# Second attention: the window branch transposed on TensorE a block later, queries asked for one head ahead

## The chip, the cores and the metric

The kernel runs on one core of a Trainium2 chip. The metric is the device time of one execution in microseconds (us). Runs of one kernel agree within some tenths of a per cent.

## The reference

One transformer layer on 1024 tokens of width 1024: a feed-forward half-step, a token mixer, a second feed-forward half-step, and a final norm. The mixer adds a differential attention (8 heads) and a sparse attention (16 heads of width 64 in 2 groups). The sparse attention is the one touched here; it is the second that the kernel computes. Cut to what matters:

```python
def nsa(q, k_cmp, v_cmp, k_slc, v_slc, k_win, v_win, gate_logits, ...):
    ...                                   # o_cmp: attention to compressed keys
    s = jnp.where(mask, q @ ks * scale, NEG_INF)       # selected blocks; 16 of 16 are selected
    o_slc = softmax(s) @ v_slc                         # so: causal attention to all tokens
    s = jnp.where(window mask, q @ kw * scale, NEG_INF) # the last WIN = 512 tokens
    o_win = softmax(s) @ v_win
    g = jax.nn.sigmoid(gate_logits)
    return g[..., 0:1] * o_cmp + g[..., 1:2] * o_slc + g[..., 2:3] * o_win
```

So each query block of 128 tokens meets two key ranges: block i has i+1 key tiles of 128 in the selected branch, and min(i+1, 5) in the window branch.

## The kernel before

The program is one stream of tile operations on one core; a scheduler places them on the engines' queues when the program is built, by its own estimate of times, and each engine then works through its queue in that order. SP issues all DMAs. The stages are: first feed-forward; preliminary projections; `da_phase`, the first (differential) attention; `ns_phase`, the second attention; projections; second feed-forward.

`ns_phase` loops over 2 groups, 4 pairs of heads each, the two halves H of the sequence, the two heads of the pair (`par`), and 4 query blocks i of the half: 128 blocks in all. For each block `ns_scores` makes, for the selected branch and then for the window branch:

- `scores` (L822 to L831): two matmuls for each piece into a PSUM tile `S` (three buffers), mask and row maximum on DVE (L829), exponential with row sums on ACT into `Ps` (selected) or `Pw` (window), two buffers each.
- the reciprocal of both row sums and the gate, in `l` (L983, L984).
- the scaled probabilities as two f16 halves, high and low, in a tile `ph` (two buffers for each branch): the high half on POOL for the selected branch (L993) and on ACT for the window branch (L991), the low half on DVE (L994).
- a DMA transpose of that tile from SBUF to SBUF (L996) into `pT` (four buffers), issued by SP.

`ns_pv` multiplies the transposed tiles with the values (`vt`, f16 with both halves side by side, L1011) into a PSUM tile `o`, three blocks later (`NS_LAG = 3`). The first product of four blocks takes the compressed branch `pc` (L1005). After four blocks `ns_fold` (L1019 on ACT, L1020 on DVE) folds `o` into `y`, and after both heads of a pair `ns_out` splits `y` and stores it (L1028). At the top of each head the queries `qt` are loaded (L1342, two tiles, two buffers each), at the top of each pair and half `pc` (L1335).

Between the blocks `fill.step()` puts pieces of independent matrix products (L51 to L53, "the filler", into `gm`) into the program: the gate projections and the first attention's output projection.

`da_phase` computes a similar attention without DMA transposes: there the probabilities are scaled on POOL (L863) and DVE (L865), transposed on PE (L877) and split from PSUM on ACT (L88) and DVE (L84).

Of the kernel before, what the change touches and what calls it, by code (L numbers as in the profile page):

```python
# [7 lines left out]
F32 = mybir.dt.float32  # L8
F32R = mybir.dt.float32r
F16 = mybir.dt.float16  # L10
AF = mybir.ActivationFunctionType
ALU = mybir.AluOpType
# [4 lines left out]
P = 128  # L17
T = 1024
TB = 512
# [3 lines left out]
KD = 8  # L23
# [63 lines left out]
def split(nc, hi, lo, src):  # L87
    nc.scalar.activation(out=hi, in_=src, func=AF.Copy)  # L88
    return lo_of(nc, lo, src, hi)


def load_w(K, src):
    if K.fill is not None:
        return K.fill.take()
    return load_w_parts(K, src, 1)()
# [171 lines left out]
def ffn_up(K, w13, w2, ctxt, ctx0, gi, first):  # L267
# [45 lines left out]
    with ctx:  # L313
# [33 lines left out]

        n0, n1 = NPLAIN, NF // 2
        r = load(n0)
        X, sv = first_product(r)  # L350
        for fp in range(n0, n1):
# [314 lines left out]
def gate_unit(K, c):  # L666
    nc = K.nc
    w = load_w(K, K.A["win"][C_GATE + c])
    for tb in range(NTB):
        ps = K.gm.tile([P, TB], F32, tag="gm", name="gm")  # L670
        yield from fill_gemm(K, ps, w, K.h[tb])
        vt = K.vtp.tile([P, TB], F32, tag="vt", name="vt")
        nc.vector.tensor_tensor(out=vt, in0=ps, in1=K.R[tb], op=ALU.mult)
        nc.sync.dma_start(out=K.s_mix[tb][c % KD][:, c // KD], in_=vt)


def pda_load(K):
    nc = K.nc
    K.y = []
    for tb in range(NTB):  # L680
        K.y.append([])
        for k in range(KD):
            t = [K.hp.tile([P, TB], F32R, tag=f"{n}{tb}_{k}", name="yl") for n in ("hi", "lo")]
            for i in range(2):
                nc.sync.dma_start(out=t[i].bitcast(F32), in_=K.s_yda[tb][k][:, i])
            K.y[tb].append(t)


def pda_unit(K, d):
    nc = K.nc  # L690
    if d == 0:
        pda_load(K)
    w = load_w(K, K.A["wda"][d])
    for tb in range(NTB):
        ps = K.gm.tile([P, TB], F32, tag="gm", name="gm")
        yield from fill_gemm(K, ps, w, K.y[tb])
        vt = K.vtp.tile([P, TB], F32, tag="vt", name="vt")
        nc.scalar.activation(out=vt, in_=ps, func=AF.Copy)
        nc.sync.dma_start(out=K.s_mix[tb][d][:, 2], in_=vt)


def compress_load(K, kv):
# [257 lines left out]
def ns_load_values(K):  # L960
    K.nv = {}
    vt = [pool.tile([P, 2, 8, P], F16, tag=tag, name="vt") for pool, tag in ((K.kp, "v0"), (K.mp, "m42"))]
    for g in range(2):
        for br in range(2):
            t = vt[g][:, br]
            K.nc.sync.dma_start(out=t, in_=K.s_v2[br][g])
            K.nv[g, br] = t


def ns_scores(K, hd, i, qt, g):  # L970
    nc = K.nc
    w = P * (i + 1)
    b0 = max(0, i - 4)
    ww = P * (i + 1 - b0)
    l = K.sm.tile([P, 2], F32, tag="l", name="l")
    nm = K.sm.tile([P, 2], F32, tag="nm", name="nm")
    qs = [t[:, (i % 4) * P:(i % 4 + 1) * P] for t in qt]
    p0 = K.pp.tile([P, T], F32, tag="P0", name="Ps")
    p1 = K.pp.tile([P, 5 * P], F32, tag="P1", name="Pw")
    scores(K, [(q, K.nk[g, 0], 0) for q in qs], w, K.slab[:, T - w:T], nm[:, 0:1], p0, l[:, 0:1])  # L980
    mk = K.slab[:, T - ww:T] if i < 4 else K.wslab
    scores(K, [(q, K.nk[g, 1], b0 * P) for q in qs], ww, mk, nm[:, 1:2], p1, l[:, 1:2])
    nc.vector.reciprocal(out=l, in_=l)  # L983
    nc.vector.tensor_tensor(out=l, in0=l, in1=K.G[:, i, hd * 3 + 1:hd * 3 + 3], op=ALU.mult)  # L984
    ts = []
    for c, (p, n) in enumerate(((p0, w), (p1, ww))):
        half = K.hp16.tile([P, n // P, 2, P], F16, tag=f"H{c}", name="ph")
        hi, lo = half[:, :, 0], half[:, :, 1]
        pv, lc = p[:, 0:n].rearrange("p (j k) -> p j k", k=P), l[:, c:c + 1]
        if c:  # L990
            nc.scalar.activation(out=hi, in_=pv, func=AF.Copy, scale=lc)  # L991
        else:
            nc.gpsimd.tensor_scalar(out=hi, in0=pv, scalar1=lc, scalar2=1.0, op0=ALU.mult, op1=ALU.mult)  # L993
        nc.vector.scalar_tensor_tensor(out=lo, in0=pv, scalar=lc, in1=hi, op0=ALU.mult, op1=ALU.subtract)  # L994
        t = K.tp.tile([P, n // P, 2, P], F16, tag=f"T{c}", name="pT")
        nc.sync.dma_start_transpose(out=t.rearrange("p j a q -> p (j a) q"), in_=half.rearrange("p j a q -> p (j a q)"))  # L996
        ts.append(t)
    return ts


def ns_pv(K, i, ts, o, pc, g, par):
# [22 lines left out]
def ns_out(K, pr, H, y):  # L1024
    nc = K.nc
    yo = K.mp.tile([P, 2, TB], F32R, tag="rl", name="yo")
    split(nc, yo[:, 0], yo[:, 1], y)
    nc.sync.dma_start(out=K.s_yns[H][pr], in_=yo.bitcast(F32))  # L1028


def order_after(K, inst, first):
    if first is not None:
        K.tc.add_manual_dep(inst.ins, first.ins.name,
                            mybir.DependencyInfo(mybir.DependencyClass.NoSync, mybir.DependencyReason.DATA),
                            reason="order the filler's weights")


class Filler:
# [22 lines left out]
    def load(self):  # L1061
        n = len(self.loaded)
        if n < len(self.srcs):
            st = self.K.wst.tile([P, KD, P], F32, tag="wst", name="wst")
            order_after(self.K, self.K.nc.sync.dma_start(out=st, in_=self.srcs[n]), self.last)
            self.loaded.append(st)

    def split(self):
# [147 lines left out]
def gate_units(K, cs):  # L1216
    return [lambda c=c: gate_unit(K, c) for c in cs]
# [22 lines left out]
NS_LAG = 3  # L1240
# [63 lines left out]
def ns_phase(K):  # L1304
    nc = K.nc
    K.low = LOW_NS
    with ExitStack() as ctx:
        K.wslab = open_pool(K, ctx, "wsl", 1).tile([P, 5 * P], F32, name="wslab")
        nc.sync.dma_start(out=K.wslab, in_=K.A["wslab"])
        K.qp, K.kp, K.pcp = open_pool(K, ctx, "nq", 2), open_pool(K, ctx, "nk", 1), open_pool(K, ctx, "npc", B_NPC)  # L1310
        K.pp, K.sm, K.tp, K.op = (open_pool(K, ctx, "np", B_NP), open_pool(K, ctx, "nsm", 6), open_pool(K, ctx, "nt", B_NT),
                                  open_pool(K, ctx, "no", B_NO))
        K.hp16 = open_pool(K, ctx, "nh", B_NH)
        K.sp = open_pool(K, ctx, "sp2", 3, True)
        K.ops = open_pool(K, ctx, "o2", 1, True)
        K.gm = open_pool(K, ctx, "gm2", 1, True)
        fill = K.filler
        fill.pace(8 + 16 + KD, PACE_NS)
        ns_load_values(K)
        pend = []  # L1320

        def finish(hd, i, res, st, g, par):
            if i % 4 == 0:
                K.o = K.ops.tile([P, TB], F32, tag="o", name="o")
            ns_pv(K, i, res, K.o, st[0], g, par)
            if i % 4 == 3:
                ns_fold(K, g, par, K.o, st[1])
                if par:
                    ns_out(K, hd // 2, i // 4, st[1])

        for g in range(2):
            for pr in range(4 * g, 4 * g + 4):
                for H in range(2):
                    pc = K.pcp.tile([P, 2, TB], F32R, tag="pc", name="pc")
                    nc.sync.dma_start(out=pc.bitcast(F32), in_=K.s_pc[pr][H])  # L1335
                    y = K.op.tile([P, TB], F32, tag="y", name="y")
                    for par in range(2):
                        hd = pr * 2 + par
                        qt = []
                        for z in range(2):  # L1340
                            t = K.qp.tile([P, TB], F32R, tag=f"q{z}", name="qt")
                            nc.sync.dma_start(out=t.bitcast(F32), in_=K.s_qns[hd // 4][z:z + 2, :, hd % 4, :, H * TB:(H + 1) * TB]  # L1342
                                              .rearrange("h a d t -> (h a) d t"))
                            qt.append(t)
                        for i in range(4 * H, 4 * H + 4):
                            res = ns_scores(K, hd, i, qt, g)
                            fill.step()
                            pend.append((hd, i, res, (pc, y), g, par))
                            if len(pend) > NS_LAG:
                                finish(*pend.pop(0))  # L1350
        fill.end()
        for p in pend:
            finish(*p)


def proj(K, open_x, after):
# [54 lines left out]
def body(tc, A, out):  # L1411
    nc = tc.nc
    K = Ctx()
    K.tc, K.nc, K.A = tc, nc, A
    K.low, K.vv, K.gate, K.fill, K.seen = 0, {}, None, None, {}
    K.h, K.acc, K.R = [None] * 2, [None] * 2, [None] * 2
    with ExitStack() as ctx:
# [172 lines left out]
```

## Time and profile before

| | |
|---|---|
| time, median of 3 runs | 3113.57 us (3110.08 to 3121.97) |
| the profiled execution's own time | 3118.4 us |
| its span in the profile | 3116.6 us |
| granted TensorE clock, mean over the span | 0.944 |
| PE busy (share of the span) | 2811.5 us (90%) |
| DVE busy | 1982.2 us (64%) |
| ACT busy | 1213.8 us (39%) |
| POOL busy | 902.3 us (29%) |
| second attention | about 1490 to 2250 us |

How to read it: PE is TensorE's matmuls, PEld its weight loads, DVE VectorE, ACT ScalarE, POOL GpSimd, SP the engine that issues the DMAs. A busy share is an average over stages with different limits; a change in one stage is read from that stage. A line such as `PE o L1011 <- DMA pT<-ph: 118.1, 66, 12.3` says that PE, before the instruction that writes `o` at line 1011, idled 118.1 us in total, 66 times, at most 12.3 us, until the DMA that fills `pT` from `ph` had landed. The granted clock is the share of full speed that TensorE got. Across the whole page PE is busy in nine tenths or more of most slices, and in five to eight tenths in the slices of the second attention.

### The profile page before, as it was taken

What the parts mean: (1) busy time and instruction counts of PE and PEld (TensorE: products, weight loads), DVE (VectorE), ACT (ScalarE), POOL (GpSimd) and SP (SyncE); (2) the same over time, 40 slices, a digit from 0 to 9 for tenths busy, and PEclk for the clock granted to TensorE, in tenths of its full rate; (3) what the DMA queues carried; (4) which work ended last, traced back from release to release, by engine and by line L of the source; (5) the groups of instructions that cost most, each with busy time, mean ns of one, the idle gap of its engine ahead of it and who ended that gap; (6) DMA issues with size and microseconds to landing.
All of it is one profiled execution on the core that took longest, in us unless ns stands there. A gap on an engine that the chain in (4) does not pass through costs nothing. (4 is left out here: it accounts for less than half of the span.)

```text
span 3116.6 us, 39466 instructions
## 1 busy us (share of the span) xinstructions
PE 2811.5 (90%) x14080; PEld 2309.3 (74%) x14080; DVE 1982.2 (64%) x3108; ACT 1213.8 (39%) x2024; POOL 902.3 (29%) x637
## 2 busy tenths in 40 slices
PE   9999999999999999898677765777899999999998
PEld 7887788887887778787566654566678788777886
DVE  8765675666784677677566664566533676576656
ACT  6322233533332454455444442445432532222443
POOL 4366550000242223222111110111152326655101
PEclk9999999999999999999778876788899999999999
DMA  3354467654456454444689888889972225545854
GB/s 135 122 202 173 176 206 266 221 160 138 150 218 211 156 181 171 171 152 149 125 169 165 166 163 214 165 159 176 215 292 106 88 102 188 174 172 187 276 199 142
DMA packets 491238, 545.32 MB, mean 175 GB/s; under 512 B 299424, under 2 KB 319136, under 8 KB 491040
## 3 DMA queue, kind: packets, MB, share of 16 engines
q1 hardware_dynamic: 491040, 542.79, 59.5%
q8 instruction: 111, 1.82, 0.2%
q14 instruction: 87, 0.71, 0.1%
HBM read 312.52 MB, written 160.96 MB: 152 GB/s over the span
## 5 line engine op out<-in xcount | busy, mean ns | idle before, releaser
L822 PE MATMUL S<-kt,qt 128*128 128x320 f32 (+5 forms) x1152 | 288.6, 374 | 85.7 <-DMA qt<-sqn 46.0
L51 PE MATMUL gm<-hi,whi 128*128 128x512 f32 x880 | 357.7, 407 | 6.6 <-ACT whi L88 3.9
L52 PE MATMUL gm<-lo,whi 128*128 128x512 f32 x880 | 353.2, 401 | 0.0
L53 PE MATMUL gm<-hi,wlo 128*128 128x512 f32 x880 | 353.0, 402 | 0.1
L822 PEld LDWEIGHTS S<-kt,qt 128*128 128x128 f32 x1152 | 210.9, 211 | 119.9 <-DMA qt<-sqn 53.9
L829 DVE CUSTOM_DVE_ANT_0 S<-S,slab 128x896 f32<-128x896 f32 (+7 forms) x320 | 224.3, 710 | 116.7 <-PE S L822 114.6
L993 POOL TENSOR_SCALAR ph<-Ps,l 128x384 f16<-128x384 f32 (+7 forms) x128 | 113.2, 885 | 623.6 <-DVE l L984 292.8
L326 PE MATMUL Y<-tf,whi 128*128 128x512 f32 x864 | 271.3, 396 | 12.7 <-DVE u L369 9.5
L1011 PE MATMUL o<-pT,vt 128*128 128x128 f16 x2112 | 170.8, 240 | 118.6 <-DMA pT<-ph 118.1
L84 DVE TENSOR_TENSOR wlo<-st,whi 128x1024 fp32r<-128x1024 f32 x154 | 197.6, 1303 | 117.5 <-ACT whi L88 117.2
L1011 PEld LDWEIGHTS <-vt 128*128 128x128 f16 x2112 | 145.1, 109 | 154.6 <-issue 153.0
L52 PE MATMUL acc<-wlo,whi 128*128 128x512 f32 (+1 forms) x628 | 242.8, 387 | 0.0
L51 PE MATMUL acc<-whi 128*128 128x512 f32 (+1 forms) x628 | 242.6, 386 | 0.0
L53 PE MATMUL acc<-whi,wlo 128*128 128x512 f32 (+1 forms) x628 | 242.3, 388 | 0.0
L88 ACT ACTIVATE whi<-st 128x1024 fp32r<-128x1024 f32 x154 | 159.9, 1056 | 187.3 <-PE acc L53 117.3
L326 PEld LDWEIGHTS Y<-tf,whi 128*128 128x128 f32 x864 | 161.8, 189 | 55.0 <-issue 10.9
L51 PEld LDWEIGHTS gm<-hi,whi 128*128 128x128 f32 x880 | 171.7, 195 | 41.3 <-ACT whi L88 4.5
L53 PEld LDWEIGHTS gm<-hi,wlo 128*128 128x128 f32 x880 | 171.0, 194 | 37.1 <-DVE wlo L84 0.6
L52 PEld LDWEIGHTS gm<-lo,whi 128*128 128x128 f32 x880 | 171.7, 195 | 32.0
L84 DVE TENSOR_TENSOR wlo<-a,whi 128x1024 fp32r<-128x1024 f32 x90 | 135.6, 1509 | 73.8 <-ACT whi L88 73.0
L84 DVE TENSOR_TENSOR wlo<-wst,whi 128x1024 fp32r<-128x1024 f32 x103 | 134.5, 1309 | 75.3 <-ACT whi L88 65.3
L326 PE MATMUL Y<-tf,wlo 128*128 128x512 f32 x432 | 170.1, 395 | 0.0
(321 smaller groups left out, 6533.5 us busy)
## 6 DMA issues: line engine op xcount, KB each, us to landing
wst<-in_win_dram SPq DMA_DIRECT2D x55, 512.0 KB
sw<-w2s SPq DMA_DIRECT2D x44, 512.0 KB
st<-sw SPq DMA_DIRECT2D x88, 256.0 KB
st<-saT SPq DMA_DIRECT2D x88, 256.0 KB
a<-in_f1w_dram SPq DMA_DIRECT2D x36, 512.0 KB
a<-in_f2w_dram SPq DMA_DIRECT2D x36, 512.0 KB
st<-saB SPq DMA_DIRECT2D x66, 256.0 KB
qt<-sq SPq DMA_DIRECT2D x128, 128.0 KB
```

The source lines that it names most:

```text
L51: first = nc.tensor.matmul(out, lhsT=w[0][:, wk], rhs=x[0], start=start, stop=False, skip_group_check=skip)
L52: nc.tensor.matmul(out, lhsT=w[0][:, wk], rhs=x[1], start=False, stop=False, skip_group_check=skip)
L53: nc.tensor.matmul(out, lhsT=w[1][:, wk], rhs=x[0], start=False, stop=stop, skip_group_check=skip)
L84: return nc.vector.tensor_tensor(out=lo, in0=src, in1=hi.bitcast(F32), op=ALU.subtract)
L88: nc.scalar.activation(out=hi, in_=src, func=AF.Copy)
L326: K.mark = nc.tensor.matmul(o, lhsT=w[a][:, m * h + k], rhs=x[k][b], start=start and k == 0 and i == 0, stop=k == h - 1 and i == 2, skip_g ...
L822: K.last = nc.tensor.matmul(S[:, o:o + n], lhsT=q, rhs=k[:, k0 + c:k0 + c + n], start=i == 0, stop=i == 1)
L829: nc.vector.tensor_tensor_reduce(out=sv, in0=sv, in1=mv, scale=-0.125, scalar=BIG, op0=ALU.add, op1=ALU.min, accum_out=nm)
L993: nc.gpsimd.tensor_scalar(out=hi, in0=pv, scalar1=lc, scalar2=1.0, op0=ALU.mult, op1=ALU.mult)
L1011: nc.tensor.matmul(dst, lhsT=K.nv[g, br][:, j], rhs=ts[br][:, j - b0, hl], start=False, stop=i % 4 == 3 and (br, j, hl) == (1, i, 1), skip ...
```

## The change

In the second attention only the selected branch is still transposed by DMA. For the window branch POOL scales the probabilities in place (f32), and a new function `ns_window` transposes them on PE, one block later, into a PSUM tile from the ring of `S`; ACT makes the high half and DVE the low half from PSUM. The loads of the queries and of `pc` move from the top of each head to the second block of the head before. The other DMAs of the stage and of the filler go through `K.dq`, which is SP's queue as before.

```diff
 def ns_scores(K, hd, i, qt, g):
-    for c, (p, n) in enumerate(((p0, w), (p1, ww))):
-        half = K.hp16.tile([P, n // P, 2, P], F16, tag=f"H{c}", name="ph")
-        ...
-        if c:
-            nc.scalar.activation(out=hi, in_=pv, func=AF.Copy, scale=lc)
-        else:
-            nc.gpsimd.tensor_scalar(out=hi, in0=pv, scalar1=lc, scalar2=1.0, op0=ALU.mult, op1=ALU.mult)
-        nc.vector.scalar_tensor_tensor(out=lo, in0=pv, scalar=lc, in1=hi, op0=ALU.mult, op1=ALU.subtract)
-        t = K.tp.tile([P, n // P, 2, P], F16, tag=f"T{c}", name="pT")
-        nc.sync.dma_start_transpose(...)
+    nb = i + 1
+    half = K.hp16.tile([P, nb, 2, P], F16, tag="H0", name="ph")
+    ...
+    nc.gpsimd.tensor_scalar(out=hi, in0=pv, scalar1=lc, scalar2=1.0, op0=ALU.mult, op1=ALU.mult)
+    nc.vector.scalar_tensor_tensor(out=lo, in0=pv, scalar=lc, in1=hi, op0=ALU.mult, op1=ALU.subtract)
+    t = K.tp.tile([P, nb, 2, P], F16, tag="T0", name="pT")
+    nc.sync.dma_start_transpose(...)
+    nc.gpsimd.tensor_scalar(out=p1[:, 0:ww], in0=p1[:, 0:ww], scalar1=l[:, 1:2], scalar2=1.0, op0=ALU.mult, op1=ALU.mult)
+    return [t, p1]
+
+def ns_window(K, i, ts):
+    nc = K.nc
+    nb = min(i + 1, 5)
+    tr = K.sp.tile([P, T], F32, tag="S", name="tr")[:, 0:nb * P].rearrange("p (j q) -> p j q", q=P)
+    for j in range(nb):
+        nc.tensor.transpose(tr[:, j], ts[1][:, j * P:(j + 1) * P], K.ident)
+    t = K.tp.tile([P, nb, 2, P], F16, tag="T1", name="wT")
+    nc.scalar.activation(out=t[:, :, 0], in_=tr, func=AF.Copy)
+    nc.vector.tensor_tensor(out=t[:, :, 1], in0=tr, in1=t[:, :, 0], op=ALU.subtract)
+    ts[1] = t
 ...
 def ns_phase(K):
+        heads = [(g, pr, H, par) for g in range(2) for pr in range(4 * g, 4 * g + 4) for H in range(2) for par in range(2)]
+        def fetch():
+            ...            # two loads of qt, and of pc if par == 0
+        fetch()
+        for n, (g, pr, H, par) in enumerate(heads):
+            ...
+            for i in range(4 * H, 4 * H + 4):
+                res = ns_scores(K, hd, i, qt, g)
+                if i % 4 == 1:
+                    fetch()
+                fill.step()
+                if pend:
+                    ns_window(K, pend[-1][1], pend[-1][2])
+                pend.append((hd, i, res, (pc, y), g, par))
+                if len(pend) > NS_LAG:
+                    finish(*pend.pop(0))
```

On PE, at the second block of a head (i = 1, scores 128x256), the queue before holds that block's scores, a piece of filler and the next block's first scores:

```order
L822 MATMUL S<-kt,qt 128x256 x4
L51 MATMUL gm<-hi,whi 128x512
L52 MATMUL gm<-lo,whi 128x512
L53 MATMUL gm<-hi,wlo 128x512
L822 MATMUL S<-kt,qt 128x384 x2
```

and now, in the same half of the sequence:

```order
L1003 MATMUL tr<-ident,Pw 128x128 x5
L822 MATMUL S<-kt,qt 128x256 x4
L51 MATMUL gm<-hi,whi 128x512
L52 MATMUL gm<-lo,whi 128x512
L53 MATMUL gm<-hi,wlo 128x512
L1003 MATMUL tr<-ident,Pw 128x128
L822 MATMUL S<-kt,qt 128x384 x4
```

The transposes of a block (`tr`, five tiles of the head before, one of this head's first block) now stand between the scores of the next block and those of the block after that.

On POOL, in a run of blocks in the middle of the stage, the queue before held one scaling for each block; in brackets is what each waits for (a DMA queue's count, DVE, ACT):

```order
L993 TENSOR_SCALAR ph<-Ps,l 128x128 [waits DMAHW5_49,DVE_49,Activation_49]
L993 TENSOR_SCALAR ph<-Ps,l 128x2x128 [waits DMAHW7_49,DVE_49,Activation_49]
L993 TENSOR_SCALAR ph<-Ps,l 128x3x128 [waits DMAHW1_49,DVE_49,Activation_49]
L993 TENSOR_SCALAR ph<-Ps,l 128x4x128 [waits DMAHW4_49,DVE_49,Activation_49]
L993 TENSOR_SCALAR ph<-Ps,l 128x5x128 [waits DMAHW6_49,DVE_49,Activation_49]
```

and now two:

```order
L990 TENSOR_SCALAR ph<-Ps,l 128x4x128 [waits DMAHW1_49,DVE_49,Activation_49]
L994 TENSOR_SCALAR Pw<-Pw,l 128x512 [waits PE_49,Activation_49]
L990 TENSOR_SCALAR ph<-Ps,l 128x5x128 [waits DMAHW5_49,DVE_49,Activation_49]
L994 TENSOR_SCALAR Pw<-Pw,l 128x640 [waits PE_49,Activation_49]
L990 TENSOR_SCALAR ph<-Ps,l 128x6x128 [waits DMAHW6_49,DVE_49,Activation_49]
```

The window's scaling (`Pw<-Pw`) stands behind the selected branch's (`ph<-Ps`), which waits for a DMA: the transpose that read the same `ph` buffer two blocks earlier.

On SP, around the loads of `pc` for one pair's second half and the next pair's first (`spc_1` and `spc_0`; what follows is a number), before:

```order
L996 DMA_TRANSPOSE pT<-ph 128x6x128 x2
L996 DMA_TRANSPOSE pT<-ph 128x8x128 x2
L1335 DMA pc<-spc_1_110 128x1024
L1342 DMA qt<-sqn_80 128x1x512 x4
L1335 DMA pc<-spc_0_111 128x1024
L1028 DMA syn_1_156<-yo 128x1024
L996 DMA_TRANSPOSE pT<-ph 128x10x128 x2
```

and now:

```order
L993 DMA_TRANSPOSE pT<-ph 128x4x128
L1352 DMA qt<-sqn_80 128x1x512 x2
L1357 DMA pc<-spc_0_111 128x1024
L993 DMA_TRANSPOSE pT<-ph 128x6x128
L993 DMA_TRANSPOSE pT<-ph 128x8x128
L993 DMA_TRANSPOSE pT<-ph 128x10x128
```

One transpose is left for each block (the middle number is twice the count of 128x128 tiles), and the next head's `qt` and `pc` stand in the middle of a head.

More of the change, by code (lines that the diff above doesn't have):

```diff
@@ L673, in gate_unit @@
         nc.vector.tensor_tensor(out=vt, in0=ps, in1=K.R[tb], op=ALU.mult)
-        nc.sync.dma_start(out=K.s_mix[tb][c % KD][:, c // KD], in_=vt)
+        K.dq.dma_start(out=K.s_mix[tb][c % KD][:, c // KD], in_=vt)
 def pda_load(K):
@@ L684, in pda_load @@
             for i in range(2):
-                nc.sync.dma_start(out=t[i].bitcast(F32), in_=K.s_yda[tb][k][:, i])
+                K.dq.dma_start(out=t[i].bitcast(F32), in_=K.s_yda[tb][k][:, i])
             K.y[tb].append(t)
@@ L698, in pda_unit @@
         nc.scalar.activation(out=vt, in_=ps, func=AF.Copy)
-        nc.sync.dma_start(out=K.s_mix[tb][d][:, 2], in_=vt)
+        K.dq.dma_start(out=K.s_mix[tb][d][:, 2], in_=vt)
 def compress_load(K, kv):
@@ L965, in ns_load_values @@
             t = vt[g][:, br]
-            K.nc.sync.dma_start(out=t, in_=K.s_v2[br][g])
+            K.dq.dma_start(out=t, in_=K.s_v2[br][g])
             K.nv[g, br] = t
@@ L985, in ns_scores @@
     ts = []
-    for c, (p, n) in enumerate(((p0, w), (p1, ww))):
-        half = K.hp16.tile([P, n // P, 2, P], F16, tag=f"H{c}", name="ph")
-        hi, lo = half[:, :, 0], half[:, :, 1]
-        pv, lc = p[:, 0:n].rearrange("p (j k) -> p j k", k=P), l[:, c:c + 1]
-        if c:
-            nc.scalar.activation(out=hi, in_=pv, func=AF.Copy, scale=lc)
-        else:
-            nc.gpsimd.tensor_scalar(out=hi, in0=pv, scalar1=lc, scalar2=1.0, op0=ALU.mult, op1=ALU.mult)
-        nc.vector.scalar_tensor_tensor(out=lo, in0=pv, scalar=lc, in1=hi, op0=ALU.mult, op1=ALU.subtract)
-        t = K.tp.tile([P, n // P, 2, P], F16, tag=f"T{c}", name="pT")
-        nc.sync.dma_start_transpose(out=t.rearrange("p j a q -> p (j a) q"), in_=half.rearrange("p j a q -> p (j a q)"))
-        ts.append(t)
-    return ts
+    nb = i + 1
+    half = K.hp16.tile([P, nb, 2, P], F16, tag="H0", name="ph")
+    hi, lo = half[:, :, 0], half[:, :, 1]
+    pv, lc = p0[:, 0:w].rearrange("p (j k) -> p j k", k=P), l[:, 0:1]
+    nc.gpsimd.tensor_scalar(out=hi, in0=pv, scalar1=lc, scalar2=1.0, op0=ALU.mult, op1=ALU.mult)
+    nc.vector.scalar_tensor_tensor(out=lo, in0=pv, scalar=lc, in1=hi, op0=ALU.mult, op1=ALU.subtract)
+    t = K.tp.tile([P, nb, 2, P], F16, tag="T0", name="pT")
+    nc.sync.dma_start_transpose(out=t.rearrange("p j a q -> p (j a) q"), in_=half.rearrange("p j a q -> p (j a q)"))
+    nc.gpsimd.tensor_scalar(out=p1[:, 0:ww], in0=p1[:, 0:ww], scalar1=l[:, 1:2], scalar2=1.0, op0=ALU.mult, op1=ALU.mult)
[10 more added lines that the diff above has]
+    ts[1] = t
 def ns_pv(K, i, ts, o, pc, g, par):
@@ L1027, in ns_out @@
     split(nc, yo[:, 0], yo[:, 1], y)
-    nc.sync.dma_start(out=K.s_yns[H][pr], in_=yo.bitcast(F32))
+    K.dq.dma_start(out=K.s_yns[H][pr], in_=yo.bitcast(F32))
 def order_after(K, inst, first):
@@ L1064, in load @@
             st = self.K.wst.tile([P, KD, P], F32, tag="wst", name="wst")
-            order_after(self.K, self.K.nc.sync.dma_start(out=st, in_=self.srcs[n]), self.last)
+            order_after(self.K, self.K.dq.dma_start(out=st, in_=self.srcs[n]), self.last)
             self.loaded.append(st)
@@ L1318, in ns_phase @@
         fill.pace(8 + 16 + KD, PACE_NS)
+        K.dq = nc.sync
         ns_load_values(K)
@@ L1329, in finish @@
                     ns_out(K, hd // 2, i // 4, st[1])
[L1331 to L1350, printed above, removed]
@@ new lines, in ns_phase @@
+        heads = [(g, pr, H, par) for g in range(2) for pr in range(4 * g, 4 * g + 4) for H in range(2) for par in range(2)]
+        ready = []
+        def fetch():
+            if len(ready) == len(heads):
+                return
+            g, pr, H, par = heads[len(ready)]
+            hd = pr * 2 + par
+            qt = []
+            for z in range(2):
+                t = K.qp.tile([P, TB], F32R, tag=f"q{z}", name="qt")
+                K.dq.dma_start(out=t.bitcast(F32), in_=K.s_qns[hd // 4][z:z + 2, :, hd % 4, :, H * TB:(H + 1) * TB]
+                               .rearrange("h a d t -> (h a) d t"))
+                qt.append(t)
+            if par == 0:
+                pc = K.pcp.tile([P, 2, TB], F32R, tag="pc", name="pc")
+                K.dq.dma_start(out=pc.bitcast(F32), in_=K.s_pc[pr][H])
+            else:
+                pc = ready[-1][1]
+            ready.append((qt, pc))
@@ new lines, in ns_phase @@
+        fetch()
+        for n, (g, pr, H, par) in enumerate(heads):
+            hd = pr * 2 + par
+            qt, pc = ready[n]
+            if par == 0:
+                y = K.op.tile([P, TB], F32, tag="y", name="y")
+            for i in range(4 * H, 4 * H + 4):
[8 more added lines that the diff above has]
+                    finish(*pend.pop(0))
@@ L1351, in ns_phase @@
         fill.end()
+        ns_window(K, pend[-1][1], pend[-1][2])
         for p in pend:
             finish(*p)
+        K.dq = nc.sync
 def proj(K, open_x, after):
@@ L1414, in body @@
     K.tc, K.nc, K.A = tc, nc, A
+    K.dq = nc.sync
     K.low, K.vv, K.gate, K.fill, K.seen = 0, {}, None, None, {}
```

## The prediction

> **What bounds the kernel now.** I read the engine table by stretches first, then the tensor engine's waits in the stage that the change touches (the second attention), then the waits of the engines that feed it, and the DMA queues. Columns of the first: start and end in us, length, busy us (and instructions) of PE, PE's weight loads, DVE, ACT, POOL, then granted clock, DMA share, GB/s. The three rows are the second attention, the first attention, and the last filler-only stretch before it.
>
> ```profile
> 1490.00:2250.00 760.00, 544.93 (x3707) 449.27 (x3707) 451.38 (x1107) 333.11 (x723) 116.42 (x131) 0.82 0.87 170
> 1000.00:1450.00 450.00, 421.56 (x2190) 355.77 (x2189) 313.28 (x641) 214.09 (x435) 118.87 (x119) 0.98 0.48 166
> 1400.00:1450.00 50.00, 48.00 (x268) 41.56 (x269) 38.17 (x84) 28.17 (x60) 13.55 (x15) 1.00 0.46 157
> ```
>
> The second attention takes 760 us. PE is busy for 544.93 of them and idle for 215.07, at a clock of 0.82; in the first attention, which transposes on PE, it idles for 28 of 450 at 0.98. Work at full clock is about 544.93 x 0.82 = 447 us, so 98 us of the busy time are slow clock. The ceiling of any gain here is 215 + 98 = 313 us. PE's waits in the stage (us in total, times, longest), and those of the engines behind it:
>
> ```profile
> PE o L1011 <- DMA pT<-ph: 118.1, 66, 12.3
> PE S L822 <- DMA qt<-sqn: 46.0, 18, 6.1
> PE o L1005 <- DVE y L1020: 21.4, 10, 4.2
> PE S L822 <- ACT Ps L831: 15.4, 11, 6.0
> PE o L1005 <- DMA pc<-spc: 7.1, 3, 4.2
> PE S L822 <- ACT Pw L831: 5.1, 8, 1.1
> POOL ph L993 <- DMA pT<-ph: 161.1, 35, 9.5
> ACT ph L991 <- DMA pT<-ph: 114.4, 51, 8.9
> DVE ph L994 <- POOL ph L993: 55.5, 39, 4.9
> ```
>
> The six PE rows add to 213.1, practically all of the 215.07. Over half is the DMA transposes, and ACT and POOL stand still for them too, because the two `ph` buffers of a branch come free only when a transpose has read them. The chain of waits of the stage says the same in its sum by line, the DMA transpose first:
>
> ```profile
> by line: DMA pT<-ph 4.9%; PE o L1011 1.9%; PE S L822 1.9%; DVE ph L994 1.2%; issue 1.2%; DVE S L829 1.0%; DMA qt<-sqn 1.0%; PE gm L51 0.9%; PE gm L52 0.9%; PE gm L53 0.8%; DMA yl<-syn 0.7%; SPq L1370 0.4%; PE o L1005 0.2%; ACT Pw L831 0.2%;
> ```
>
> The DMA engines in the stage, and the transposes on SP's own queue (min/median/max ns):
>
> ```profile
> DMA packets 303508, 129.15 MB, mean 170 GB/s; under 512 B 280652, under 2 KB 280652, under 8 KB 303452
> q1 hardware_dynamic: 303452, 128.45, 86.6%
> L996 SPq DMA_TRANSPOSE pT<-ph x256: 1169/1388/6172, 1503.9 to 2241.7; - x128
> ```
>
> So DMA is 87% busy, and the change takes from that.
>
> **The change, part by part.**
>
> *Window transposes leave the DMA.* Per head the blocks i = 0 to 7 have i+1 tiles of 128x128 in the selected branch (36) and min(i+1, 5) in the window (30), each in two halves: 16 x 72 = 1152 and 16 x 60 = 960 half-tiles of 32,768 bytes, together 69.2 MB of the stage's 129.15. The other 59.9 MB are 79 GB/s over 760 us; by the stretch 1400 to 1450, which has no transposes (0.46 at 157 GB/s), they take 0.46 x 79/157 = 0.23 of the engines. The transposes take 0.866 - 0.23 = 0.635, or 483 us: 0.229 us for each half-tile. The 960 removed ones are 219 us, and DMA falls from 658 to 439 us. SP loses 128 issues of at least 1.17 us, 150 us, with their waits. [...]
>
> *What comes instead on PE.* 480 transposes (16 x 30). In the first attention seven stand together, and four:
>
> ```profile
> 1334.68 0.93 PE L877 MATMUL tr<-ident,Pt 128*128 128x128 f32 x7
> 1335.36 0.71 PE L822 MATMUL S<-kt,qt 128*128 128x128 f32 x4
> ...
> 1339.96 0.60 PE L877 MATMUL tr<-ident,Pt 128*128 128x128 f32 x4
> 1340.31 0.36 PE L899 MATMUL o<-th,vt 128*128 128x256 f32 x1
> ...
> L877 PE MATMUL tr<-ident,Pt 128*128 128x128 f32 x252 | 38.8, 275 | 0.2 <-DVE m L918 0.2
> ```
>
> From start to the next one's start seven take 0.68 us, 0.097 each: 47 us for 480 (busy time of the group, 38.8/252 = 0.154, would make it 74; the next instruction already runs then, so I take 47). PE's work becomes 494 us at full clock.
>
> *The split moves to other engines.* Today the window's high half is ACT (L991), its low half DVE (L994), from SBUF; after it POOL scales the tile first, then ACT and DVE split the transpose out of PSUM, as they do in the first attention:
>
> ```profile
> L994 DVE SCALAR_TENSOR_TENSOR ph<-Pw,l,ph 128x640 f16<-128x640 f32 x64 | 57.8, 905 | 14.3 <-ACT ph L991 14.3
> L991 ACT ACTIVATE ph<-Pw,l 128x640 f16<-128x640 f32 x64 | 52.9, 826 | 74.5 <-DMA pT<-ph 58.4 <-DVE l L984 7.3 <-ACT Pw L831 4.9
> ...
> L84 DVE TENSOR_TENSOR tl<-tr,th 128x512 fp32r<-128x512 f32 x42 | 28.7, 684 | 4.4 <-ACT th L88 4.2
> L88 ACT ACTIVATE th<-tr 128x512 fp32r<-128x512 f32 x42 | 24.7, 596 | 59.3 <-PE tr L877 57.6 <-DVE nm L829 1.7
> L84 DVE TENSOR_TENSOR tl<-tr,th 128x384 fp32r<-128x384 f32 x28 | 15.4, 551 | 2.4 <-ACT th L88 2.2
> L88 ACT ACTIVATE th<-tr 128x384 fp32r<-128x384 f32 x28 | 13.7, 490 | 23.3 <-PE tr L877 23.2
> L863 POOL TENSOR_SCALAR Pt<-Pt,l 128x640 f32<-128x640 f32 x8 | 6.4, 805 | 49.0 <-DVE l L862 49.0
> ```
>
> Extended by their slopes to 640 columns these are 817 ns on DVE (905 today) and 702 on ACT (826): 6 and 8 us less over the 64 wide blocks. DVE is left with about 446 us, ACT with 325. DVE's 446 of 612 would be 0.73, a little over the 0.70 of the first attention (313.28/450); held to 0.70 it would make the stage 637 us, which the range covers. POOL gains at most 128 x 0.805 = 103 us, 219 of 760. None of this is on PE's path except through latency: a transpose waits for POOL's scaling, which stands on POOL behind the selected branch's scaling, which waits for a transpose DMA two blocks older. Behind a held PE transpose stand the scores of the next block but one. What that wait costs the trace of before doesn't show. Its ends: 0.2 us, the first attention's L877 row; 55.5 us, DVE's waits for POOL's `ph`, a handover with nothing between. I take 20: the order puts the scores of another block between, as in the first attention, but fewer filler matmuls than there. PSUM's three `S` buffers now serve three uses for each block instead of two; the `Ps` and `Pw` waits (20.5 us) I leave as they are.
>
> *Queries and `pc` a head ahead.* They are asked for in the second block of the head before, three blocks before use; at 760/128 = 5.9 us a block, or somewhat less, that is some 15 us, and the longest wait was 6.1. The 46.0 and 7.1 us go to 0 (ends 0 and 53.1). The tail, the `K.dq` lines (still SP's queue) and the rest of the program cost nothing: same instructions.
>
> *What stays.* `y` 21.4, `Ps` and `Pw` 20.5: 42 us. Of the 118.1 us for `pT` the selected branch's transposes remain, with DMA at 439 of some 610 us, 0.72 instead of 0.866, and three blocks of lag; ends 0 and 118, I take a quarter, 30. PE's idle time is 42 + 30 + 20 = 92 us.
>
> *The clock.* It falls after long gaps, not after short ones:
>
> ```profile
> 1969.85 0.72 PE L1011 MATMUL o<-pT,vt 128*128 128x128 f16 x10 [2.06 <-DMA pT<-ph]
> 1971.16 0.39 PE L52 MATMUL gm<-yl,whi 128*128 128x512 f32 x1
> ...
> 1977.20 1.65 PE L1011 MATMUL o<-pT,vt 128*128 128x128 f16 x14 [5.07 <-DMA pT<-ph]
> 1979.40 0.63 PE L51 MATMUL gm<-yl,whi 128*128 128x512 f32 x1
> 1981.53 0.63 PE L53 MATMUL gm<-yl,wlo 128*128 128x512 f32 x1
> 1983.56 0.39 PE L51 MATMUL gm<-yl,whi 128*128 128x512 f32 x1
> ```
>
> After 2.06 us of idling a filler matmul still lasts 0.39 us; after 5.07 us it lasts 0.63 for over 4 us. The removed waits are the long ones (12.3, 6.1), so I take 0.95, between 0.82 here and 0.98 in the first attention: 494/0.95 = 520 us.
>
> *Sum.* 520 + 92 = 612 us against 760: 148 us less. The profiled execution took 3118.4 us (span 3116.6), 4.8 above the median of 3113.57; 3118.4 - 148 = 2970, and against the median 3113.57 - 148 = **2965 us**.
>
> **The rivals.**
>
> *More falls away.* `pT` goes to 10 and the new wait to 0, clock 0.98: 494/0.98 + 52 = 556, total 2910. For it: the first attention's shape. Against it: there PE has more filler for each block of scores.
>
> *The selected branch keeps half of the stall.* Its 1152 half-tiles are the larger part. In blocks 4 to 7, with 13 of them on average, DMA needs 13 x 0.229 + 180/128 = 4.4 us a block, close to PE's share there. Half of `pT` (59), 40 for the new wait, clock 0.88: 561 + 59 + 42 + 40 = 702, total 3056. For it: POOL's 161.1 us behind these buffers, of which two stay.
>
> *PE transposes are dear.* At the row's own 275 ns each, if they didn't overlap, 480 are 132 us: (447 + 132)/0.95 + 92 = 701, total 3055; with a clock of 0.90 besides, 735 and 3089. Against it: the starts 0.097 us apart, and the clock of 0.98 with 252 of them. [...]
>
> *Slower.* The chain POOL, PE, scores: PE now waits in its queue for the transpose DMA through POOL's order, as well as three blocks later in the products. If `pT` keeps its 118 us and the clock its 0.82, with queries gone: 494/0.82 + 118 + 42 + 20 = 782 us, 22 more than now, total 3136. It decides once PE idles for more than 760 - 602 = 158 us at that clock. For it: POOL's waits average 161.1/35 = 4.6 us, long enough to drop the clock. Against it: 219 of 658 us of DMA work are gone.
>
> **How the numbers follow.** The forecast 0.62 (its own range 2920 to 3020), more falling away 0.12, half of the stall 0.14, dear transposes 0.04, slower 0.08. The range from 2905 to 3060 leaves out the slower case, most of the dear one and what lies below the first rival, under 0.2. A change within 0.5% (16 us) can hardly be told from none here; faster by more than that gets 0.90, the same 0.04, slower 0.06: slices of the half-stall and slower cases lie near zero.
>
> **What would show it.** In the profile after: the stage at about 612 us; DMA share in it near 0.72, with 122,880 small packets fewer (960 x 128); PE's `qt` and `pc` waits gone; `pT` near 30; a group of 480 `tr` matmuls about 0.1 us apart with some 20 us of idling ahead, ended by POOL; granted clock near 0.95. It is wrong if PE idles over 130 us in the stage, if the clock stays under 0.9, or if another wait (`S` for ACT, `ph` for POOL) takes the 118 us over.

## The result, and the profile after

The changed kernel takes 3094.81 us (median, 3092.13 to 3099.65) against 3115.02 us for the kernel before in the same comparison: a ratio of 0.993 (95% interval 0.9913 to 0.9947). It is faster, by 20 us and not by 148. The profiled execution took 3095.32 us, its span is 3093.5 us.

The second attention now ends near 2230 instead of 2250. Its row in the table of stretches (columns as before: start and end, length, busy of PE, PE's weight loads, DVE, ACT, POOL, then clock, DMA share, GB/s), and PE's waits in it:

```profile
1490.00:2230.00 740.00, 573.00 (x4177) 480.74 (x4177) 469.80 (x1107) 321.72 (x724) 193.07 (x259) 0.89 0.69 132
```

```profile
PE o L1020 <- DMA pT<-ph: 138.7, 39, 8.2
PE tr L1003 <- POOL Pw L994: 9.1, 14, 2.3
PE S L822 <- ACT Pw L831: 4.3, 5, 1.2
PE o L1014 <- DVE y L1029: 4.1, 5, 1.8
PE tr L1003 <- DVE wT L1006: 3.2, 5, 1.5
...
PE o L1014 <- DMA pc<-spc: 1.1, 1, 1.1
```

Three things stand out. The wait for queries has gone altogether, as forecast. The new wait of the transposes on POOL is small. But the wait for the transposed probabilities, which was 118.1 us in 66 waits, is 138.7 us in 39: fewer and longer, although the transposing DMA has lost nearly half of its tiles. PE idles for 167 us (740 - 573), and the clock is 0.89.

The chain of waits of the stage says which of these ends last. First its sum by line (1490 to 2250), then three of its pieces between 1707 and 1742 (start, us, what):

```profile
by line: DMA pT<-ph 37.7%; PE o L1020 13.5%; PE S L822 9.7%; issue 4.2%; PE tr L1003 4.0%; DVE S L829 3.9%; PE gm L51 3.9%; PE gm L52 3.5%; PE gm L53 3.2%; DVE ph L991 2.8%; POOL ph L990 1.8%; DMA yl<-syn 1.7%; DVE wT L1006 1.5%; ACT Pw L83
```

```profile
1707.71 8.79 DMA pT<-ph
1728.01 3.69 DMA pT<-ph
1733.18 8.41 DMA pT<-ph
```

The timeline shows what stands just ahead of the long ones. First SP's own queue, then PE (start, duration, instruction, and in brackets the idle time before it):

```profile
1705.73 1.17 SPq L1352 DMA_DIRECT2D qt<-sqn  x2
1707.12 0.33 SPq L1357 DMA_DIRECT2D pc<-spc  x1
1707.71 2.00 SPq L993 DMA_TRANSPOSE pT<-ph  x1
...
1730.45 1.49 SPq L1352 DMA_DIRECT2D qt<-sqn  x2
1732.12 0.45 SPq L674 DMA_DIRECT2D smx<-vt  x1
1733.18 8.79 SPq L993 DMA_TRANSPOSE pT<-ph  x2
```

```profile
1710.57 0.60 PE L1003 MATMUL tr<-ident,Pw 128*128 128x128 f32 x4
1716.53 0.80 PE L1020 MATMUL o<-pT,vt 128*128 128x128 f16 x6 [5.37 <-DMA pT<-ph]
```

The transposes that take 8 to 9 us were issued right behind a pair of query loads. The one at 1728.01, which was not, took 3.69. Over the whole stage PE waits for `pT` 29 times for more than 2 us, 129 of the 138.7 us, and 26 of these waits end 8 to 15 us after a head's two query loads were issued. That is the theory that the experiments test.

### The profile page after: what moved, and what is told of

It reads as the page before. It is cut to its first block, busy times and chain, and to the rows that moved or that the text cites. A ratio compares the mean times of both kernels' runs of the same rounds, so it can differ in the third digit from the quotient of the medians.

```text
span 3093.5 us, 40468 instructions
## 1 busy us (share of the span) xinstructions
PE 2840.9 (92%) x14560; PEld 2344.8 (76%) x14560; DVE 2001.4 (65%) x3108; ACT 1202.4 (39%) x2024; POOL 979.4 (32%) x765
## 2 busy tenths in 40 slices
DMA packets 364265, 513.91 MB, mean 166 GB/s; under 512 B 172448, under 2 KB 192160, under 8 KB 364064
## 3 DMA queue, kind: packets, MB, share of 16 engines
q1 hardware_dynamic: 364064, 511.32, 55.4%
## 4 chain that ended last, share of the span: by engine, by line
PE 62%; DMA 18%; DVE 11%; POOL 3%; issue 3%; ACT 2%; SPq 1%; DVEq 0%; POOLq 0%; ACTq 0%
DMA pT<-ph 9%; PE gm L51 5%; PE gm L52 5%; PE gm L53 5%; PE Y L326 5%; PE acc L53 5%; PE acc L51 5%; PE acc L52 5%; PE S L822 4%; PE o L1020 3%; PE X L326 3%; PE Z L326 3%; DVE w2s L434 2%; DVE wlo L84 2%; DVE S L829 1%
## 5 line engine op out<-in xcount | busy, mean ns | idle before, releaser
L822 PE MATMUL S<-kt,qt 128*128 128x320 f32 (+5 forms) x1152 | 279.1, 369 | 25.2 <-ACT Pt L831 10.7
L990 POOL TENSOR_SCALAR ph<-Ps,l 128x384 f16<-128x384 f32 (+7 forms) x128 | 102.8, 803 | 507.5 <-DVE l L984 250.1
L822 PEld LDWEIGHTS S<-kt,qt 128*128 128x128 f32 x1152 | 199.9, 206 | 42.2 <-ACT Pt L831 12.2
L1020 PE MATMUL o<-pT,vt 128*128 128x128 f16 x1152 | 100.7, 241 | 138.9 <-DMA pT<-ph 138.7
L991 DVE SCALAR_TENSOR_TENSOR ph<-Ps,l,ph 128x384 f16<-128x384 f32 (+7 forms) x128 | 130.1, 1017 | 71.5 <-POOL ph L990 70.8
```

Of the source, the lines that this page charges most:

```text
L822: K.last = nc.tensor.matmul(S[:, o:o + n], lhsT=q, rhs=k[:, k0 + c:k0 + c + n], start=i == 0, stop=i == 1)
L1020: nc.tensor.matmul(dst, lhsT=K.nv[g, br][:, j], rhs=ts[br][:, j - b0, hl], start=False, stop=i % 4 == 3 and (br, j, hl) == (1, i, 1), skip ...
```

## The experiments

**Theory A.** A query tile is loaded by one DMA whose source is `(h a) d t`: four groups of 32 rows, so that its outer size (the count of its slowest dimension) is four. The theory supposes, as its author's estimate, that it runs on 4 of the 16 DMA engines, for several us, that a transpose uses all 16 and lands with its last one, and that so a transpose behind such a load waits for those four, and PE for the transpose. Its 104 GB/s for a load is what the changed kernel's DMA moved from 1712.50 to 1714.00 us, while such a load ran. **Theory B:** the two `ph` buffers hold the loop. **Theory C:** the lag of three blocks is too short in PE's new order.

### The load in four pieces

```diff
-K.dq.dma_start(out=t.bitcast(F32), in_=K.s_qns[hd // 4][z:z + 2, :, hd % 4, :, H * TB:(H + 1) * TB]
-               .rearrange("h a d t -> (h a) d t"))
+for j in range(4):
+    K.dq.dma_start(out=t[j * 32:(j + 1) * 32].bitcast(F32),
+                   in_=K.s_qns[hd // 4][z + j // 2, j % 2, hd % 4, :, H * TB:(H + 1) * TB])
```

The same bytes in the same 2-KB rows, but the outer size of each piece is 32.

> Each query tile is loaded by four DMAs of 32 partitions instead of one of 128 partitions whose source has four groups of rows. Theory A: a query load moves at about 104 GB/s (a quarter of the engines) for some 5 us, and the transpose issued behind it, that of the third block of each head, lands 4 to 5 us later for it; 32 heads times 4 us is the 139 us that PE waits for pT. By A the wait for pT falls from 139 to 20 to 50 us and the time from 3095 to 2980 to 3020 us. Theory B: the two ph buffers hold the loop of scaling, transpose and scaling two blocks on, whatever the queries do; then the wait for pT stays over 110 us and the time within 10 us of 3095. Theory C: PE's order asks for pT too early (three blocks of lag), whatever the queries do: as B.

Measured: 2946.83 us, ratio 0.9473 (0.9457 to 0.9488), better than A's range. Its stretch and PE's waits (the stage ends near 2093):

```profile
1490.00:2090.00 600.00, 519.97 (x4116) 426.49 (x4115) 465.48 (x1094) 314.87 (x711) 197.24 (x259) 0.99 0.66 157
```

```profile
PE o L1020 <- DMA pT<-ph: 34.3, 38, 2.6
PE tr L1003 <- POOL Pw L994: 18.6, 21, 2.4
PE o L1014 <- DVE y L1029: 8.7, 8, 2.1
PE tr L1003 <- DVE wT L1006: 5.9, 7, 1.8
PE S L822 <- ACT Pw L831: 4.7, 10, 0.8
```

Nothing but the shape of a load has changed, and 104 of the 138.7 us are gone, the longest wait falls from 8.2 to 2.6 us, and the clock returns to 0.99. B and C, which this edit leaves as they are (the same two buffers, the same lag), are not what held the changed kernel.

### No loads at all

Queries are loaded for the first head only, and the 31 later heads use the same tiles: their loads are left out (and with them the later heads' own queries), the rest of the work is the same.

```diff
-qt = []
-for z in range(2):
+qt = [] if not ready else ready[0][0]
+for z in range(2 if not ready else 0):
```

> Queries are loaded for the first head only and reused by all others, which leaves 31 of 32 query loads out. A: the wait for pT falls to 10 to 40 us, the time to 2970 to 3010 us. B and C: the time stays at 3080 to 3100 us, since the loads are hidden already.

Measured: 2945.35 us, ratio 0.9464 (0.9446 to 0.9482); the wait for `pT` is 40.0 us. The time is again below A's range, and the split kernel's time within the uncertainty: the loads in four pieces cost nothing that can be measured, and the loads in one piece cost the changed kernel some 145 us (0.993 - 0.9464 of about 3112).

### Which engines the load holds

Two experiments separate "it stands in the same queue" from "it holds four engines". In the first, ScalarE's queue issues the loads:

```diff
-K.dq.dma_start(out=t.bitcast(F32), ...)
+nc.scalar.dma_start(out=t.bitcast(F32), ...)
```

> The changed kernel with the query loads issued by ScalarE's queue and not by SyncE's; each is still one load of four groups. If A holds because the transpose stands in the same queue of each engine behind the load's packets, it now stands in another, and the wait on transposed probabilities goes from 138.7 us to 30 to 70: 2960 to 3020 us. If A holds because the four engines are themselves taken, whichever queue the packets come from, it stays at 110 to 140: 3060 to 3100. If B or C holds: 3085 to 3105.

Measured: 3114.55 us, ratio 1.0013 (0.9995 to 1.0031). PE's wait:

```profile
PE o L1020 <- DMA pT<-ph: 144.7, 45, 6.2
```

Both numbers are somewhat over the second case's ranges; the first case, the order in one queue, falls. The kernel has a second use: the loads now have a DMA queue of their own (q10), so the page shows what they take. The DMA queues from 1498.3 to 1504.7 us, while one head's two loads ran (packets, MB, share of the time of 16 engines):

```profile
q1 hardware_dynamic: 690, 0.17, 78.6%
q10 hardware_dynamic: 262, 0.52, 23.7%
```

In 6.4 us the load took 23.7% of 16 engines, which is 3.8 of them, and both tiles (0.52 MB) were through at its end. Over another head, 6.0 us from 1642.7, it is 24.7%; in other heads the packets of the two loads spread over up to 11.5 us. Two loads that ran on different engines at once would together have shown more than four. Over the 32 heads 6 us each are at least some 190 us in which 3.8 engines were taken, a figure that the mean share of 0.69 does not show. That a piece of 32 rows gets 16 is the theory's estimate; no share was measured for it.

A share alone can't tell four engines held from sixteen held for a quarter of the time, but the packet counts can help. A head's queries are 256 rows of 2 KB, and the 8,448 packets of q10 are 264 for each of 32 heads: 8 small ones more, 4 for each load. The split kernel has 3,840 packets more than the changed kernel's 364,064 in q1, which makes 128 small ones a head, 16 for each of its 8 loads. The number of small packets goes with the number of engines that the theory gives to a load.

The second makes two loads out of one, by halves, so that each source has two groups:

```diff
+for j in range(2):
+    K.dq.dma_start(out=t[j * 64:(j + 1) * 64].bitcast(F32),
+                   in_=K.s_qns[hd // 4][z + j, :, hd % 4, :, H * TB:(H + 1) * TB])
```

> The changed kernel with each query tile brought in by two loads of 64 partitions, whose source has an outer size of two. Theory A by the number of engines: each load runs on 2 engines, one behind the other or both on the same two, so that the same bytes take twice as long, 10 us a head, and hold the transpose up by more: 3150 to 3250 us. If instead what helped in x1 is that the pieces are smaller: between the changed kernel and x1, 2980 to 3060.

Measured: 3219.74 us, ratio 1.0345 (1.0321 to 1.037), in A's range. PE's wait over the stage, which now lasts to 2360:

```profile
PE o L1020 <- DMA pT<-ph: 256.0, 44, 11.8
```

Four pieces made the kernel some 145 us faster, two made it some 125 us slower. That the pieces are smaller can't explain both; a number of engines that goes 4 (3.8 by the share), 16 (the theory's estimate), 2 (1.9 to 2.1 packets in flight, below) does. The count of packets is the changed kernel's 364,064 again, 2 small ones for each of a head's 4 loads. In the record of the single packets, where a head's loads stand by themselves, their 2-KB packets are mostly 1.9 to 2.1 in flight on average, for 11 to 13 us; in the changed kernel mostly 3.7 to 4.0, for 6 to 7 us. A transpose that runs by itself in the changed kernel has 18.4 of its 256-byte packets in flight, and 1233 start in 1.5 us (from 1729.5); beside a load it has 18.0 in flight, and 2 start in 2 us (from 1712.5). The longest wait grows from 8.2 to 11.8 us.

### Each part of the change, with either load

Two kernels make one part of the change alone. "Window only" leaves the loads at the top of the head; "fetch only" leaves both branches on DMA:

```diff
-fetch()
 for n, (g, pr, H, par) in enumerate(heads):
+    fetch()                     # window only: here, and not in the second block of the head before
     ...
-    if i % 4 == 1:
-        fetch()
```

> The window branch on TensorE, but queries and pc asked for at the top of each head as before. A: PE waits for qt again (30 to 60 us) and the transposes behind the loads are late as well, at another block; the time is 3095 to 3150 us. B and C: the wait for qt adds to an unchanged wait for pT: 3130 to 3150 us. By the prediction's own sum it would be 2965 + 53 = 3018 us.

Measured: 3099.83 us, ratio 0.9962 (0.9945 to 0.998).

```profile
PE o L1020 <- DMA pT<-ph: 137.3, 41, 7.5
PE S L822 <- DMA qt<-sqn: 5.5, 2, 3.8
```

PE waits only 5.5 us for queries, so the fetch ahead was not needed for the queries to be there in time: A's time holds, its 30 to 60 us for the queries missed.

> Queries and pc one head ahead, both branches still transposed by DMA. By the prediction's sum 53 us less than before, 3062 us. A: the loads now stand ahead of transposes that two branches wait for, so that the wait for qt goes and the wait for pT grows by as much or more: 3100 to 3160 us. B and C: 3060 to 3080 us.

Measured: 3071.29 us, ratio 0.9868 (0.985 to 0.9886).

```profile
PE S L822 <- DMA qt<-sqn: 72.7, 27, 5.5
PE o L1011 <- DMA pT<-ph: 71.0, 42, 8.1
```

A missed here, in the time and in the waits: `pT` fell from 118.1 and `qt` rose from 46.0. The time lies in the range of B and C, but with other waits than theirs. The two parts together are slower than the fetch alone.

Then the same with the load in four pieces: in the kernel before, and in the changed kernel without one or the other part. The edits are those shown above, put together.

> The kernel before, its query loads at the top of the head as they were, but each query tile brought in by four loads of 32 partitions. Theory A (the load of four groups runs on 4 of the 16 DMA engines for about 5 us and holds up what needs them behind it): the load is short, so the wait for queries goes from 46.0 us to under 15, and of the 118.1 us on the transposed probabilities 30 to 60 go too, since both branches still use the DMA engines 0.76 of the stage: 3000 to 3060 us. Theory B and C (the two buffers of the halves, or the lag of three blocks, hold the loop): the queries' wait alone goes, 118 stays: 3065 to 3090.

Measured: 3034.7 us, ratio 0.9744 (0.9718 to 0.9771). PE's waits (before: `pT` 118.1, `qt` 46.0):

```profile
PE o L1011 <- DMA pT<-ph: 91.6, 70, 14.1
PE S L822 <- DMA qt<-sqn: 7.9, 6, 1.9
```

The time is in A's range. No row of the stage shows the 0.76 that the expectation takes for the DMA engines; their share in it was 0.87 before and is 0.86 here. The load's shape was there before the change and cost some 75 us there, of which 38 are the wait for queries and 26 the wait for `pT`, a little less than A's 30 to 60. Whether the 91.6 us that stay come from the transposes' own load, which the prediction names, is not shown: the last kernel of this section has the same transposes and waits 39.2 us for them.

> Window branch through TensorE, query loads split in four, but at the top of the head: the change without its fetch ahead, beside x1 (2946.8 us) which has it. If the fetch ahead earns nothing once the load is short (x5 waits 7.9 us for queries with the load at the top): 2945 to 2965 us, and the wait for queries under 10 us. If the load's lead still matters: 2970 to 3000, the wait for queries 20 to 46.

Measured: 2958.52 us, ratio 0.9513 (0.9498 to 0.9529); the wait for queries is 3.1 us. Both are in the first case's ranges: with the short load the fetch ahead earns some 12 us beside the window part.

> Both branches through the DMA engines as before, query loads split in four and a head ahead: the change without its window part, beside x5 (3034.7 us), which has neither part. If the gain of x1 over x5, 88 us, is the window's alone: 3020 to 3040 us. If the fetch carries a part of it: 2960 to 3015. The transposed probabilities' wait stays near x5's 91.6 us by the first, and falls to 50 to 75 by the second.

Measured: 3005.96 us, ratio 0.9667 (0.9651 to 0.9684).

```profile
PE S L822 <- DMA qt<-sqn: 40.1, 39, 2.1
PE o L1011 <- DMA pT<-ph: 39.2, 37, 8.1
```

Neither line of the expectation is met in full: the fetch does carry a part, and `pT` falls further than said.

All eight together, in us, with the ratio to the kernel before in the same comparison (whose median was between 3108 and 3115):

| | load of four groups | load in four pieces |
|---|---|---|
| neither part | 1 | 3034.7 (0.9744) |
| fetch ahead only | 3071.3 (0.9868) | 3006.0 (0.9667) |
| window on PE only | 3099.8 (0.9962) | 2958.5 (0.9513) |
| both | 3094.8 (0.993) | 2946.8 (0.9473) |

By the ratios, at 0.01 for 31 us: down the right column the change is worth 84 us; the window brings 72 by itself and the fetch 24. Down the left the window brings 12 by itself, and added to the fetch it loses 19. PE's waits for `pT` and `qt` together say where it goes: down the left column they are 164.1, 143.7, 142.8 and 138.7 us, down the right 99.5, 79.3, 42.0 and 34.3. With the load of four groups they stay near 140 us whichever part is made; with the load in pieces the window's part takes more than half of them off. That four held engines are the limit which both parts of the change meet is the reading that fits this, with the experiments above. Why the queries are waited for in the two "fetch only" kernels, 27 and 39 times, was not settled.

### What still stands in the way

POOL now scales the window's tile while DVE subtracts the selected branch's halves. The groups of the changed kernel (us busy, mean ns, then idle before):

```profile
L991 DVE SCALAR_TENSOR_TENSOR ph<-Ps,l,ph 128x384 f16<-128x384 f32 (+7 forms) x128 | 130.1, 1017 | 71.5 <-POOL ph L990 70.8
L994 POOL TENSOR_SCALAR Pw<-Pw,l 128x640 f32<-128x640 f32 (+4 forms) x128 | 90.1, 704 | 20.9 <-DVE l L984 16.6 <-PE S L822 4.2
```

Before, the same subtraction took 826 ns. In the split kernel the scaling was moved to ScalarE:

```diff
-nc.gpsimd.tensor_scalar(out=p1[:, 0:ww], in0=p1[:, 0:ww], scalar1=l[:, 1:2], scalar2=1.0, op0=ALU.mult, op1=ALU.mult)
+nc.scalar.activation(out=p1[:, 0:ww], in_=p1[:, 0:ww], func=AF.Copy, scale=l[:, 1:2])
```

> The split load of x1 with the scaling of the window's probabilities moved from GpSimd to ScalarE. Theory: GpSimd's scaling runs beside VectorE's subtraction and slows both (the subtraction 1017 ns after, 826 before); with it gone the subtraction comes back to 830 to 900, the wait of TensorE's transposes on GpSimd (18.6 us) goes, and ScalarE has some 128 x 0.5 us more: 2910 to 2945 us against 2947. Rival: ScalarE, in order, now runs the scaling ahead of the exponentials of the next block, and TensorE waits for its score buffers instead: 2950 to 2990.

Measured: 2946.98 us (2935.79 to 2948.4), ratio 0.946 (0.9434 to 0.9487): the same as with POOL, and between the ranges of the theory and of its rival.

```profile
L991 DVE SCALAR_TENSOR_TENSOR ph<-Ps,l,ph 128x384 f16<-128x384 f32 (+7 forms) x128 | 104.2, 814 | 41.2 <-POOL ph L990 39.8 <-DMA qt<-sqn 0.6
```

```profile
PE o L1020 <- DMA pT<-ph: 46.2, 39, 4.6
PE tr L1003 <- ACT Pw L994: 6.7, 12, 1.2
```

POOL's scaling did slow the subtraction: 1019 ns in the split kernel, 814 here, and the wait of PE's transposes for the scaling falls from 18.6 to 6.7 us. But PE waits 12 us more for `pT`, and the time stays: by these two rows the gain turned into another wait. With a third buffer for the halves on top:

```diff
-B_NH = 2
+B_NH = 3
```

> x8 (split load, window scaled by ScalarE) with three buffers for the halves instead of two. x8 still waits 46.2 us on transposed probabilities, and GpSimd waits for a buffer of the halves. Theory B (the buffers are what now holds the transpose back): that wait goes to 10 to 25 us and the time to 2920 to 2940. Rival: the transpose itself and the lag hold it, and the time stays within 2940 to 2950.

Measured: 2938.54 us (2935.59 to 2944.22), ratio 0.945 (0.9435 to 0.9466). It is the lowest median of the study, 5.5% under the kernel before, but its interval overlaps those of the split kernel and of the one with ScalarE. The time is in theory B's range, but `pT` stays at 45.6 us, so its 10 to 25 missed: the buffers do not set that wait here either. What does was not tried; the kernel without query loads still has 40.0 us of it.

## Why the prediction was wrong

- **What bounds the kernel.** Right as far as it went: PE's idle time and the slow clock were the reserve. With the long waits gone the stage takes about 607 us (the split kernel, from its first product with `pc` to its last with `wT`), against 612 predicted.
- **Window transposes off the DMA.** Right in count: 299,424 packets under 512 bytes fell to 172,448, the 122,880 of the tiles and 4,096 more, 32 for each DMA removed. The DMA share is 0.69, against 0.72, but that is luck: 0.69 of 740 us are 511 us, where the prediction had 439 in a stage of 612. What went wrong is the reading of it: the share is a mean over 16 engines, and the prediction took it for the state of each.
- **480 transposes on PE.** Right in the main, as the split kernel's timeline shows, where five stand ahead of the scores:

```profile
1703.95 0.71 PE L1003 MATMUL tr<-ident,Pw 128*128 128x128 f32 x5
1704.41 1.17 PE L822 MATMUL S<-kt,qt 128*128 128x512 f32 x4
```

  From start to start five take 0.46 us, 0.092 each (0.097 predicted), with the clock at 0.99. The rival by which such transposes are dear falls. PE's work at full clock is 573.00 x 0.89 = 510 us in the changed kernel and 515 in the split one, against 494: it grew by 63 to 68 us and not by 47, a smaller miss whose cause was not sought.
- **The split on other engines.** The two operations out of PSUM were sized well: at 640 columns they take 817 ns on DVE and 701 on ACT, forecast 817 and 702. DVE's total was not: 469.80 us in place of 446. The missing term is the subtraction of the selected branch, slower by 191 ns (1017 less 826) in 128 instances, 24 us, beside POOL's scaling.
- **The new wait on POOL.** 9.1 us, and 18.6 in the split kernel, within the ends 0.2 and 55.5; the 20 taken fits the split kernel.
- **Queries a head ahead.** The 46.0 us of waiting for queries did go to 0. But the prediction costed the loads at nothing, because they would come early enough for their reader. It named no other work that uses the engines while the load runs. In the changed kernel the load stands right in front of a transpose, and that transpose paid for its 6 us and more on four engines. The window-only kernel shows that the place at the top of the head is no better (137.3 us): the cause is the load's shape, which no step of the prediction priced.
- **`pT` at 30 us.** This is the step that failed: it came from the mean share and the lag, with nothing for the query loads, and it is 138.7. With the load in four pieces it is 34.3, near the forecast. That share and lag are what sets it then is not shown: with both branches on DMA, a share of 0.88, the same lag, and the load in pieces and a head ahead, it is 39.2.
- **The clock.** 0.89 instead of 0.95 goes with the same waits: those that stayed are the long ones, up to 8.2 us. In the split kernel none is over 2.6 us and the clock is 0.99. The 4.6 us that the rival "slower" calls long enough to drop the clock are POOL's; on PE the kernel before has a gap of 4.73 us (to 1770.17), after which the filler's matmuls last 0.63 us, and one of 2.91 us (to 2158.10), after which they last 0.39.

The sum makes the miss plain: busy time 573 instead of 520 (16 us more work, some 37 from the clock), idle time 167 instead of 92 (`pT` 109 more than forecast, everything else 34 less). These 128 us are the stage's 740 less 612. Of the rivals, "the selected branch keeps half of the stall" came nearest in its sign and its place, but named another cause, and the rival "slower" had the right row: `pT` keeping its 118 us. The prediction's own test, over 130 us of idling or a clock under 0.9, told it wrong on both.

## What to carry to other kernels

Before a load is costed at nothing because it is early, ask how many DMA engines it runs on and for how long, and what needs those engines meanwhile: here a load with an outer size of four (0.52 MB in 6.4 us) took 3.8 engines of 16, and the transposes issued behind it took 8 to 9 us, against 3.69. The mean DMA share, 0.69, did not show this; the transfers that took far longer than their like, and what was issued just ahead of them, did. And where two parts of a change meet at one hidden limit, take the limit away first: here one edit to a load was worth some 145 us in the changed kernel, and the planned change 20 without it.

## What the runs showed of the hardware

- A head's two query loads (0.52 MB in rows of 2 KB, outer size four) took 3.8 of 16 DMA engines for 6.4 us; issuing them from another engine's queue did not free the transposes behind it (144.7 us of waiting against 138.7).
- The DMA share did not measure the work done. Packet times overlap: over the 8 us from 1734 in the changed kernel the share is 1.28. And the fetch-only kernel shows 0.98 in its stretch, the kernel before with the load in pieces 0.86 at more bytes a second:

```profile
1490.00:2090.00 600.00, 435.13 (x2989) 354.10 (x2989) 378.00 (x940) 276.44 (x607) 94.15 (x110) 0.85 0.98 177
```

```profile
1490.00:2090.00 600.00, 459.79 (x3220) 378.46 (x3220) 402.60 (x989) 290.71 (x638) 102.59 (x118) 0.87 0.86 187
```

- DVE's subtraction took 1017 to 1027 ns in kernels where POOL scales the window's tile behind its own scaling (1017 in the changed kernel, 1019 in the split one, 1027 in the split one without the fetch ahead), and 814 where ScalarE does it instead.
